# Shorter slot lists, packed overflow and three dense blocks first, in the expert product of a one-core kernel

## The chip, the cores and the metric

One core of one Trainium2 chip runs the kernel. The metric is the device time of one execution in microseconds (us); "before" is the median of three timed runs, and one further execution was taken by the hardware profiler. Engines are named as the profile names them: PE (TensorE matmul), DVE (VectorE), ACT (ScalarE), POOL (GpSimd), SP (SyncE, here a queue of transfers).

## The reference

256 tokens of width 2048 pass one layer: an attention and recurrence sub-layer, then the sub-layer that matters here, PEER, which retrieves experts (16,384 of them, each one row of u and one row of v):

```python
def peer(h, w_q, sub_keys, u, v):
    ...
    gate = jax.nn.softmax(best_s, axis=-1)
    def block(args):
        hb, eb, gb = args
        ub = u[eb]
        vb = v[eb]
        act = jax.nn.gelu(jnp.einsum('td,ted->te', hb, ub).astype(jnp.float32), approximate=False) * gb
        return jnp.einsum('te,ted->td', act.astype(vb.dtype), vb)
```

Each token has 8 heads with 16 experts each, so of the 16,384 gated hidden values of a token at most 128 are not zero. A gated residual and a last RMSNorm follow.

## The kernel before, in words

The kernel computes PEER densely first and sparsely second. Experts are numbered (j, p): 128 blocks j of 128 partitions p. For each j, `stacked_block` makes the hidden values of all 256 tokens on PE, and `u_evac` (L1055) adds two halves (ACT `low`, DVE `low`) and applies GELU. `gating` multiplies the blocks j < NS by the gates, which earlier code scattered into a table, and writes them to `hid` in DRAM; blocks j >= NS stay in SBUF in `late` and are gated there (`late_gates`, L1227).

A chunk is one pair (j, p): one hidden row of 256 tokens (two tiles of 128) and one row of v with 2048 values. `make_lists` (L1106) builds for each partition p two lists of j whose chunk isn't zero: list 0 has those of tile 0, with those that both tiles use in front; list 1 those of tile 1 alone. DVE does it in turns of eight (MAX, MATCH_REPLACE, then `decode` into rows of `hid` and `w_v`). Lists have SLOTS places. What is over goes to further chunks by a place computed over all partitions: `ob` holds counts of what is over, a matmul with a triangle of ones (`ps_list`, L1187) sums them over partitions, and `spilling` (L1341) writes each item of overflow to its place in a table in DRAM by a scatter.

`second_product` (L1365) multiplies. Its items come from `plan` (L1401): "feed" items are whole late blocks whose v rows come by the queue of weight loads; a double is one slot of list 0 for both tiles; a single is one slot for one tile; "over" is a packed chunk; two dense late blocks come last. `fetch` (L1294) loads slot n of all 128 partitions at once by two indirect transfers from POOL, `hr` (128x256 of `hid`) and `v` (128x2048 of `w_v`); AHEAD = 4 items are in flight over five buffers. `parts_of` splits values in a high part (ACT `vh`, `ap`) and a low one (DVE `vl`, `ap`); `v_products` then does three matmuls of 128x512 for each of four column groups, so 12 for one tile and 24 for two:

```python
    def v_products(out, tt, q, parts, start, stop, keep=lambda i: i):
        ...
        keep(mm(out, ap[:, 0, t], vh[:, w], start, False))
        keep(mm(out, ap[:, 0, t], vl[:, w], False, False))
        keep(mm(out, ap[:, 1, t], vh[:, w], False, stop))
```

All sums stay in eight banks `out..` of PSUM until `finish` (L1455) does the last two items, residual, norm and store. One scatter is issued per item (L1388), since each engine runs its instructions in program order and POOL has the gathers too. If overflow doesn't fit, a flag `bad` makes all 128 dense blocks run as a fallback. NS = 124, SLOTS = (56, 35), BOTH = 29 and OVER = (16, 12, 10) give 2 feed items, 29 doubles, 62 singles, 2 "over" and 2 dense: 33 of 24 matmuls and 64 of 12.

## Time and profile before

| | us |
|---|---|
| median of 3 runs (2154.59, 2158.49, 2158.61) | 2158.49 |
| the profiled execution | 2151.07 |
| its span in the trace | 2149.2 |
| PE busy | 2035.7 (95%) |
| DVE busy | 1644.7 (77%) |
| ACT busy | 1068.9 (50%) |
| POOL busy | 1025.7 (48%) |

The mean granted clock of PE was 0.98. Busy times are sums over the whole span: the second product fills about its last sixth, from 1763 us on, and the work before it is the attention sub-layer, the routing and the 128 blocks of hidden values. An engine that is busy most of the time isn't thereby the one that is waited for; that is read by stage. Row starts below are microseconds from the start of the span, and a row with "[9.94 <-ACT ap L225]" says how long its engine sat idle before it and which instruction ended that.

### The profile page before, as it was taken

What the parts mean: (1) busy time and instruction counts of PE and PEld (TensorE: products, weight loads), DVE (VectorE), ACT (ScalarE), POOL (GpSimd) and SP (SyncE); (2) the same over time, 40 slices, a digit from 0 to 9 for tenths busy, and PEclk for the clock granted to TensorE, in tenths of its full rate; (3) what the DMA queues carried; (4) which work ended last, traced back from release to release, by engine and by line L of the source; (5) the groups of instructions that cost most, each with busy time, mean ns of one, the idle gap of its engine ahead of it and who ended that gap; (6) DMA issues with size and microseconds to landing.
All of it is one profiled execution on the core that took longest, in us unless ns stands there. A gap on an engine that the chain in (4) does not pass through costs nothing. (4 is left out here: it accounts for less than half of the span.)

```text
span 2149.2 us, 34359 instructions
## 1 busy us (share of the span) xinstructions
PE 2035.7 (95%) x12916; PEld 1841.5 (86%) x12916; DVE 1644.7 (77%) x2538; ACT 1068.9 (50%) x1559; POOL 1025.7 (48%) x663
## 2 busy tenths in 40 slices
PE   6989999999999999999999999998999989999996
PEld 6988998779999999899888888887888778886885
DVE  7899888878675888887999666687558776765687
ACT  3433334455645445444666555543554445654575
POOL 3333422224420001218777688777871026777763
PEclk8999999999999999999999999999999999999998
DMA  6878778676677899857777898899879979999994
GB/s 252 310 267 317 258 254 288 207 239 210 214 236 263 312 334 326 310 176 183 180 181 186 231 262 257 249 324 291 223 212 360 319 261 334 282 261 268 386 382 178
DMA packets 208832, 568.65 MB, mean 265 GB/s; under 512 B 57585, under 2 KB 89489, under 8 KB 191633
## 3 DMA queue, kind: packets, MB, share of 16 engines
q1 hardware_dynamic: 147248, 441.38, 59.5%
q0 software_dynamic: 58928, 123.94, 21.5%
q8 instruction: 103, 1.69, 0.3%
q10 hardware_dynamic: 2482, 1.07, 0.2%
q14 instruction: 71, 0.58, 0.1%
HBM read 544.95 MB, written 38.06 MB: 271 GB/s over the span
## 5 line engine op out<-in xcount | busy, mean ns | idle before, releaser
L90 ACT ACTIVATE hi<-raw 128x1024 fp32r<-128x1024 f32 x550 | 580.9, 1058 | 686.0 <-PE ps_w L120 270.6
L94 DVE TENSOR_TENSOR lo<-raw,hi 128x1024 fp32r<-128x1024 f32 x506 | 652.5, 1292 | 256.0 <-ACT hi L90 254.3
L120 PE MATMUL ps_w<-h,hi 128*128 128x512 f32 (+1 forms) x2560 | 811.9, 373 | 12.7 <-ACT hi L90 7.4
L120 PE MATMUL ps_w<-h,lo 128*128 128x256 f32 x2304 | 649.5, 282 | 10.5 <-DVE lo L94 10.5
L921 POOL DMA_INDIRECT gtab<-gate,addr x256 | 508.7, 1987 | 174.9 <-issue 70.9
L120 PEld LDWEIGHTS ps_w<-h,hi 128*128 128x128 f32 x2560 | 465.0, 189 | 100.1 <-ACT hi L90 9.2
L120 PEld LDWEIGHTS ps_w<-h,lo 128*128 128x128 f32 x2304 | 437.0, 190 | 17.4 <-DVE lo L94 16.6
L120 PE MATMUL out<-vh,ap 128*128 128x512 f32 x1008 | 313.3, 391 | 2.8 <-ACT vh L225 2.8
L226 DVE TENSOR_TENSOR vl<-v,vh 128x1024 fp32r<-128x1024 f32 x190 | 224.6, 1224 | 72.7 <-ACT vh L225 70.7
L94 POOL TENSOR_TENSOR lo<-raw,hi 128x1024 fp32r<-128x1024 f32 x44 | 117.6, 2673 | 294.1 <-ACT hi L90 294.1
L120 PEld LDWEIGHTS out<-vh,ap 128*128 128x128 f32 x1008 | 189.5, 188 | 44.4 <-ACT vh L225 5.3
L225 ACT ACTIVATE vh<-v 128x1024 fp32r<-128x1024 f32 x190 | 189.8, 1047 | 72.4 <-DMA v<-w_v,index 67.7
L120 PE MATMUL set<-h1hi,hi 128*128 128x256 f32 x768 | 212.3, 291 | 13.5 <-ACT h1hi L242 7.1
L120 PE MATMUL set<-h1hi,lo 128*128 128x256 f32 x768 | 198.5, 293 | 22.1 <-DVE lo L94 18.9
L120 PE MATMUL set<-h1lo,hi 128*128 128x256 f32 x768 | 212.8, 288 | 0.9 <-DVE h1lo L244 0.9
L120 PE MATMUL out<-vl,ap 128*128 128x512 f32 x504 | 197.6, 392 | 4.9 <-DVE vl L226 4.9
L186 DVE SCALAR_TENSOR_TENSOR raw<-raw,cond 128x1024 f32<-128x1024 f32 x96 | 134.2, 1404 | 49.6 <-DMA raw<-w_ada 45.9
L120 PEld LDWEIGHTS set<-h1hi,hi 128*128 128x128 f32 x768 | 150.1, 198 | 16.6 <-ACT h1hi L242 7.3
L120 PEld LDWEIGHTS set<-h1hi,lo 128*128 128x128 f32 x768 | 141.2, 199 | 26.6 <-DVE lo L94 23.1
L120 PE MATMUL ps_w<-h1hi,hi 128*128 128x256 f32 x528 | 150.8, 286 | 3.0 <-ACT hi L90 3.0
L120 PE MATMUL ps_w<-h1hi,lo 128*128 128x256 f32 x528 | 150.3, 285 | 1.9 <-DVE lo L94 1.9
L120 PEld LDWEIGHTS set<-h1lo,hi 128*128 128x128 f32 x768 | 150.9, 197 | 1.2 <-DVE h1lo L244 1.2
(356 smaller groups left out, 3196.6 us busy)
## 6 DMA issues: line engine op xcount, KB each, us to landing
raw<-w_u SPq DMA_DIRECT2D x256, 512.0 KB, 4.4
raw<-w_sets SPq DMA_DIRECT2D x96, 512.0 KB, 5.4
raw<-w_ada SPq DMA_DIRECT2D x96, 512.0 KB, 5.1
raw<-w_t SPq DMA_DIRECT2D x66, 512.0 KB, 4.6
ada<-w_ada SPq DMA_DIRECT2D x32, 1024.0 KB, 8.3
raw<-w_s SPq DMA_DIRECT2D x32, 512.0 KB, 4.6
gtab<-zeros_d SPq DMA_DIRECT2D x32, 512.0 KB, 5.5
raw<-w_up SPq DMA_DIRECT2D x32, 512.0 KB, 4.7
```

The source lines that it names most:

```text
L90: self.nc.scalar.activation(hi, raw, AF.Copy)
L94: i = eng.tensor_sub(lo, raw, hi.bitcast(F32))
L120: return nc.tensor.matmul(out, lhsT, rhs, start=start, stop=stop, skip_group_check=True)
L186: return nc.vector.scalar_tensor_tensor(w, w, 1.0, cond[:, k0:k0 + n], op0=ALU.mult, op1=ALU.mult, accum_out=col)
L225: nc.scalar.activation(hi, v, AF.Copy)
L226: (lo_eng or nc.vector).tensor_sub(lo, v, hi.bitcast(F32))
L921: return nc.gpsimd.indirect_dma_start(out=gtab[tt].rearrange("p (x o) -> (p x) o", o=1), out_offset=bass.IndirectOffsetOnAxis(ap=addr[:, t ...
```

## The change

NS becomes 125, so three late blocks are left, and all three are "feed" items at the front; no dense block stands at the end. Lists get 72 and 48 places (WIDE), but only the first 52 and 28 are slots that are fetched directly, and BOTH falls to 20. What is over is packed into 10 further chunks (MORE = 3 for tile 0, 7 for tile 1). The items are 3 feed, 20 doubles (the last two at the very end) and 70 singles (10 of them packed): 23 of 24 matmuls and 70 of 12, and 90 gathered chunks where there were 93.

The 38 scatters and their table go. In their place the whole lists are stored once to `table` in DRAM (from SP), and for each packed chunk and partition the source is found by products: `hot` marks, for each partition, which overflow places its items take (compares on DVE against an iota, both kept in the not yet used `ye`); 17 small matmuls (`picked`, into bank `ps_sel`) add up, for each place, partition and slot; DVE turns this into rows of `table` (`oplace`), and `picking` gathers 128 index pairs per packed chunk from POOL, one gather per item. Since `ps_sel` needs a bank, bank `out13` is taken only after it, and six matmuls of the first two feed items are held until then. The lists themselves are made after `ps_list`, not before. `late_gates` loads its gates from SP, not POOL.

```diff
-NS = 124
-SLOTS = (56, 35)
-BOTH = 29
-OVER = (16, 12, 10)
+NS = 125
+SLOTS = (52, 28)
+BOTH = 20
+WIDE = (72, 48)
+MORE = (3, 7)
...
+
+    index_all = kp.tile([P, sum(WIDE), 2], U32, name="index_all")
+    index = [index_all[:, 0:WIDE[0], :], index_all[:, WIDE[0]:, :]]
+    oplace = kp.tile([P, sum(MORE)], U32, name="oplace")
+    oindex = kp.tile([P, sum(MORE), 2], U32, name="oindex")
...
-    over = dram.tile([256 + P * sum(OVER), 2], U32, name="over")
+    ROWS = P * sum(WIDE)
+    table = dram.tile([ROWS + 1, 2], U32, name="table")
...
+
+        place = w1(sum(MORE), "place")
+        for c in range(sum(MORE)):
+            nc.vector.tensor_scalar(place[:, c:c + 1], tcol, 128.0 * (c - (c >= MORE[0]) * MORE[0]) - ROWS, None, op0=ALU.add)
+        begin = lists.tile([P, 3, 2], F32, name="begin")
+        nc.vector.memset(begin, 1.0)
+        for i, n in enumerate((SLOTS[0], WIDE[0] + SLOTS[1], BOTH)):
+            nc.vector.tensor_scalar(begin[:, i, 0:1], tcol, float(sum(WIDE)), float(n), op0=ALU.mult, op1=ALU.add)
...
-        turn_of(0, 0)
-        turn_of(0, 8)
-        decode(0, 0, 16)
-        yield 3000
...
-        nc.vector.tensor_mul(key[:, 1, :], alone, rev)
-        turn_of(1, 0)
-        decode(1, 0, 8)
-        yield 1700
-        for c in (8, 16, 24):
-            turn_of(0, 8 + c)
-            turn_of(1, c)
-            decode(0, 8 + c, 16 + c)
-            decode(1, c, c + 8)
-            yield 2500
...
         nc.vector.tensor_reduce(cnt[:, 0:1], b[:, 0, :], axis=AX.X, op=ALU.add)
         nc.vector.tensor_reduce(cnt[:, 1:2], alone, axis=AX.X, op=ALU.add)
         nc.vector.tensor_reduce(cnt[:, 2:3], both, axis=AX.X, op=ALU.add)
         ob = w1(4, "ob")
...
+        for i, n in enumerate(WIDE):
+            nc.vector.tensor_scalar(t1[:, i:i + 1], cnt[:, i:i + 1], float(n), None, op0=ALU.is_gt)
+        nc.vector.tensor_add(ob[:, 3:4], t1[:, 0:1], t1[:, 1:2])
+        yield 3000
         yield LATER
         ps = bank("ps_list")
         mm(ps[:, 0:4], tri, ob, True, True)
@@ -1189,55 +1164,93 @@
         nc.scalar.activation(off, ps[:, 0:8], AF.Copy)
         state["counted"] = True
-
-        for i in range(2):
-            for c in range(40 - 8 * i, SLOTS[i] + OVER[i], 8):
-                turn_of(i, c)
-                yield 650
-            decode(i, 40 - 8 * i, SLOTS[i] + OVER[i])
...
+        def turn_of(i, c0):
...
+        turn_of(0, 0)
+        turn_of(1, 0)
+        yield 3200
...
+        wide = 128 * max(MORE)
+        iota_w = state["space"][:, 0:wide]
+        pin(nc.gpsimd.iota(iota_w, pattern=[[1, wide]], base=0, channel_multiplier=0, allow_small_or_imprecise_dtypes=True))
...
+        end = w1(3, "end")
+        nc.vector.tensor_add(end, off[:, 0:3], ob[:, 0:3])
+        nc.vector.tensor_sub(begin[:, :, 0], begin[:, :, 0], off[:, 0:3])
+        hot = []
+        for i in range(3):
+            n = 128 * MORE[i > 0]
+            t = state["space"][:, 1024 * (i + 1):1024 * (i + 1) + n]
+            nc.vector.tensor_scalar(t, iota_w[:, 0:n], off[:, i:i + 1], None, op0=ALU.is_ge)
+            nc.vector.scalar_tensor_tensor(t, iota_w[:, 0:n], end[:, i:i + 1], t, op0=ALU.is_lt, op1=ALU.mult)
+            hot.append(t)
             yield 1000
...
+        state["hot"] = (hot, begin, place)
...
+        for i in range(2):
+            nc.vector.tensor_scalar(tot[:, i:i + 1], off[:, 4 + i:5 + i], 128.0 * MORE[i], None, op0=ALU.is_gt)
...
-        for i, n in enumerate(OVER):
...
-            nc.vector.tensor_add(oplace[i], at, dump)
+        yield 500
+        for c in range(8, WIDE[0], 8):
+            if c < WIDE[1]:
+                turn_of(1, c)
+                yield 1000
+            turn_of(0, c)
             yield 1300
-        state["placed"] = True
+        pin(nc.sync.dma_start(table[0:ROWS].rearrange("(p c) x -> p c x", p=P), index_all))
+        state["tabled"] = True
+
+    def picked(ps):
+
+        hot, begin, place = state["hot"]
+        for c in range(sum(MORE)):
+            ones = [(0, c)] if c < MORE[0] else [(1, c - MORE[0]), (2, c - MORE[0])]
+            for i, (l, n) in enumerate(ones):
+                pin(mm(ps[:, 2 * c:2 * c + 2], hot[l][:, 128 * n:128 * n + 128], begin[:, l, :],
+                       i == 0, i == len(ones) - 1))
+        got = lists.tile([P, sum(MORE), 2], F32, name="got")
+        nc.scalar.activation(got.rearrange("p c x -> p (c x)"), ps[:, 0:2 * sum(MORE)], AF.Copy)
+        nc.vector.tensor_mul(place, place, got[:, :, 1])
+        nc.vector.tensor_add(place, place, got[:, :, 0])
+        nc.vector.tensor_scalar(oplace, place, float(ROWS), None, op0=ALU.add)
 
     def late_gates():
 
-        while state["gated"] < 2:
+        while state["j"] < NS - 8:
...
+        for tt in range(2):
+            after_all(pin(nc.sync.dma_start(lateg[:, tt, :, :], gtab[tt][:, 128 * NS:])), tt)
...
         if j == 122:
-            feed.add([a["w_v"][n][:, 1024 * u:1024 * u + 1024] for n in range(NS, 126) for u in range(2)])
+            feed.add([a["w_v"][n][:, 1024 * u:1024 * u + 1024] for n in range(NS, 128) for u in range(2)])
...
+    state["space"] = ye.rearrange("p z d -> p (z d)")
...
-    def spilling():
...
-        for i, n in enumerate(OVER):
-            for k in range(n):
-                src = index[i][:, SLOTS[i] + k, :] if i < 2 else index[0][:, BOTH + k, :]
-                one = pin(nc.gpsimd.indirect_dma_start(
-                    out=over, out_offset=bass.IndirectOffsetOnAxis(ap=oplace[i][:, k:k + 1], axis=0),
-                    in_=src, in_offset=None))
...
-        got = pin(nc.sync.dma_start(oindex, over[0:256].rearrange("(c p) x -> p c x", p=P)))
...
+    def picking():
+
+        while not state["tabled"]:
+            yield
+        for c in range(sum(MORE)):
+            pin(nc.gpsimd.indirect_dma_start(
+                out=oindex[:, c, :], out_offset=None, in_=table,
+                in_offset=bass.IndirectOffsetOnAxis(ap=oplace[:, c:c + 1], axis=0)))
+            state["picked"] = True
+            yield
     def second_product(items, listed=False):
-        outs = [[bank(f"out{tt}{q}") for q in range(4)] for tt in range(2)]
+        sel = bank("ps_sel") if listed else None
+        outs = [[bank(f"out{tt}{q}") if not listed or tt == 0 or q < 3 else None for q in range(4)] for tt in range(2)]
...
-        spill = spilling() if listed else iter(())
+        pick = picking() if listed else iter(())
+        held = []
...
                 bg.run(700)
-                if state["placed"]:
-                    next(spill, None)
+                next(pick, None)
...
             for hf in range(2):
                 for tt in now[2]:
                     for q in (2 * hf, 2 * hf + 1):
-                        v_products(outs[tt][q], tt, q, now, (tt, q) in fresh, False)
-                        fresh.discard((tt, q))
+                        if outs[tt][q] is None:
+                            held.append((now, tt, q))
+                        else:
+                            take(now, tt, q)
+            if listed and n == 1:
+                while "hot" not in state:
+                    bg.run(1e9)
+                picked(sel)
+                outs[1][3] = bank("out13")
+                for h in held:
+                    take(*h)
         last = [nxt, parts_of(got.popleft())]
         finish(outs, last)
...
         two = [(1, n, (1,)) for n in range(SLOTS[1])]
-        single = []
+        single = two[:8]
+        two = two[8:]
         while one or two:
             for l in (one, two):
                 if l:
                     single.append(l.pop(0))
+        single += [("more", n, (int(n >= MORE[0]),)) for n in range(sum(MORE))]
         double = [(0, n, (0, 1)) for n in range(BOTH)]
-        dense = [("all", n, (0, 1)) for n in range(NS, 128)]
-        items, acc = [("feed", n, (0, 1)) for n in range(NS, 126)], 0.0
-        for d in double:
+        for d in double[:-2]:
             items.append(d)
-            acc += len(single) / len(double)
+            acc += len(single) / (len(double) - 2)
             while acc >= 1.0 and single:
                 items.append(single.pop(0))
                 acc -= 1.0
-        return items + single + [("over", n, (n,)) for n in range(2)] + dense[-2:]
+        return items + single + double[-2:]
```

On PE the place between the first product's last blocks (`ps_w`) and the second's first (`out`). Before:

```order
L120 MATMUL ps_w<-h_9294,hi 128x512
L120 MATMUL ps_w<-h_9294,lo 128x256
L120 MATMUL ps_list<-ob,tri 128x4
L120 MATMUL ps_list<-ob,ones_l 128x4
L120 MATMUL out_18153<-hi,ap 128x512
L120 MATMUL out_18153<-lo,ap 128x512
```

Now:

```order
L121 MATMUL ps_w<-h_9294,hi 128x512
L121 MATMUL ps_w<-h_9294,lo 128x256
L121 MATMUL ps_list<-ob,tri 128x4
L121 MATMUL ps_list<-ob,ones_l 128x4
L121 MATMUL ps_w<-h_9293,hi 128x512
L121 MATMUL ps_w<-h_9293,lo 128x256
```

The two matmuls of `ps_list` stood behind block 127; now they stand behind block 126, ahead of block 127.

On ACT the same place (`hi` are weights' high parts, `low` and `late` the last blocks' hidden values, `ap` and `vh` high parts for the second product, `off` the copy of `ps_list`, `got` that of `ps_sel`). Before:

```order
L1059 ACTIVATE low<-ps_w 128x256
L1190 ACTIVATE off<-ps_list 128x8
L1065 ACTIVATE late<-low 128x256
L225 ACTIVATE vh<-v 128x1024 x2
L225 ACTIVATE ap<-late 128x256 x2
L225 ACTIVATE ap<-hr 128x256
```

Now:

```order
L226 ACTIVATE ap<-late 128x256
L1068 ACTIVATE late<-low 128x256
L226 ACTIVATE ap<-late 128x256
L1165 ACTIVATE off<-ps_list 128x8
L91 ACTIVATE hi<-raw 128x1024 x2
L1062 ACTIVATE low<-ps_w 128x256
L91 ACTIVATE hi<-raw 128x1024
L1068 ACTIVATE late<-low 128x256
L226 ACTIVATE vh<-v 128x1024 x6
L91 ACTIVATE hi<-raw 128x1024
L226 ACTIVATE ap<-late 128x256
L1237 ACTIVATE got<-ps_sel 128x20
```

The split of the first late blocks moved ahead of every gathered `vh`; that of the last one and one `hi` of its v rows stand behind six `vh`.

On POOL the first gathers, now:

```order
L1196 IOTA ye 128x896
L1321 DMA hr<-hid,index_all 128x256
L1321 DMA v<-w_v,index_all 128x2048
L1321 DMA hr<-hid,index_all 128x256
L1321 DMA v<-w_v,index_all 128x2048
L1360 DMA oindex<-table,oplace 128x2
L1321 DMA hr<-hid,index_all 128x256
L1321 DMA v<-w_v,index_all 128x2048
L1360 DMA oindex<-table,oplace 128x2
```

Three gathered chunks stand ahead of the iota, so five ahead of the first index gather; the scatters, which stood one ahead of each of 38 items, are gone.

## Rows read from the trace of the kernel before

**Rows 1.** The page, part 1: busy us, share of the span and instructions of each engine.

```profile
PE 2035.7 (95%) x12916; PEld 1841.5 (86%) x12916; DVE 1644.7 (77%) x2538; ACT 1068.9 (50%) x1559; POOL 1025.7 (48%) x663
```

**Rows 2.** Table by stage: window; its us; busy us of each engine; PEclk, DMA share, GB/s.

```profile
1763.00:1834.00 71.00, 70.95 (x301) 58.25 (x302) 51.39 (x87) 39.77 (x54) 46.85 (x41) 0.96 0.93 337
1834.00:1934.00 100.00, 100.00 (x443) 82.81 (x442) 64.97 (x75) 55.34 (x74) 78.31 (x70) 1.00 0.99 273
1934.00:2020.00 86.00, 80.70 (x344) 63.58 (x343) 52.02 (x59) 45.00 (x60) 66.16 (x57) 1.00 0.98 305
```

**Rows 3.** Instructions that write tile out, on PE: duration ns min/median/max, first and last start.

```profile
L120 PE MATMUL out<-vh,ap x1008: 387/389/796, 1774.0 to 2132.4; 128*128 128x512 f32 x168
L120 PE MATMUL out<-vl,ap x504: 387/389/632, 1774.2 to 2132.2; 128*128 128x512 f32 x168
```

**Rows 4.** Timeline of PE, 2042 to 2056: start, us, instruction.

```profile
2042.45 0.39 PE L120 MATMUL out<-vl,ap 128*128 128x512 f32 x1
...
2054.01 0.39 PE L120 MATMUL out<-vl,ap 128*128 128x512 f32 x1
```

**Rows 5.** Timeline of ACT, 2090 to 2106: start, us, instruction, idle before and its releaser.

```profile
2093.79 2.02 ACT L225 ACTIVATE vh<-v 128x1024 fp32r<-128x1024 f32 x2 [0.68 <-DMA v<-w_v,index]
...
2102.39 2.01 ACT L225 ACTIVATE vh<-v 128x1024 fp32r<-128x1024 f32 x2 [0.66 <-DMA v<-w_v,index]
```

**Rows 6.** Timeline of POOL, 1822 to 1830 and 1976 to 1990.

```profile
1826.71 1.02 POOL L1347 DMA_INDIRECT over<-index,oplace  x1 [0.30 <-issue]
...
1984.50 1.00 POOL L1347 DMA_INDIRECT over<-index,oplace  x1 [0.31 <-issue]
...
1987.08 1.01 POOL L1307 DMA_INDIRECT v<-w_v,index  x1 [0.30 <-DVE vl L226]
1988.39 1.00 POOL L1347 DMA_INDIRECT over<-index,oplace  x1 [0.30 <-issue]
```

**Rows 7.** What PE waited for from 1826 to 1992: us in total, times, longest.

```profile
PE out L120 <- DVE vl L226: 4.1, 6, 0.8
PE out L120 <- ACT vh L225: 0.9, 1, 0.9
```

**Rows 8.** Timeline of PE, 1746.9 to 1770.

```profile
1747.06 0.39 PE L120 MATMUL ps_w<-h,hi 128*128 128x512 f32 x1
...
1752.61 0.28 PE L120 MATMUL ps_list<-ob,tri 128*128 128x4 f32 x2
1752.75 0.36 PE L120 MATMUL ps_list<-ob,ones_l 128*128 128x4 f32 x2
1763.05 0.80 PE L120 MATMUL out<-hi,ap 128*128 128x512 f32 x1 [9.94 <-ACT ap L225]
...
1768.34 0.41 PE L120 MATMUL out<-hi,ap 128*128 128x512 f32 x1
```

**Rows 9.** Timeline of ACT, 1747 to 1764.

```profile
1760.69 2.00 ACT L225 ACTIVATE vh<-v 128x1024 fp32r<-128x1024 f32 x2 [3.57 <-DMA v<-w_v,index]
1762.60 0.71 ACT L225 ACTIVATE ap<-late 128x256 fp32r<-128x256 f32 x2
```

**Rows 10.** Timeline of DVE, 1748 to 1762.

```profile
1749.76 0.41 DVE L1060 TENSOR_TENSOR low<-low,ps_w 128x256 f32<-128x256 f32 x1
...
1751.09 1.21 DVE L94 TENSOR_TENSOR lo<-raw,hi 128x1024 fp32r<-128x1024 f32 x1
1752.21 0.09 DVE L1144 MATCH_VALUE_LOAD key<-lst,key 128x8 f32 x1
```

**Rows 11.** Transfers by issue: engine, operation, count, KB each, median us to landing.

```profile
out<-ye SPq DMA_DIRECT2D x8, 256.0 KB, 2.7
...
v<-w_v,index POOLq DMA_INDIRECT x91, 8.8
```

**Rows 12.** Timeline of PE, 2111 to 2150.

```profile
2116.38 2.17 PE L120 MATMUL out<-vh,ap 128*128 128x512 f32 x4 [1.91 <-ACT vh L225]
...
2132.39 0.39 PE L120 MATMUL out<-vh,ap 128*128 128x512 f32 x1
```

More of the change, by code (lines that the diff above doesn't have):

```diff
@@ new lines, in make_lists @@
+        lst = [w1(n, f"lst{i}") for i, n in enumerate(WIDE)]
+        def turn_of(i, c0):
+            c1 = c0 + 8
+            l = lst[i][:, c0:c1]
+            nc.vector.max(l, key[:, i, :])
+            if c1 < WIDE[i]:
+                nc.vector.match_replace(key[:, i, :], l, key[:, i, :], 0.0)
+            if i == 0:
+                nc.vector.tensor_scalar(w[:, c0:c1], l, 128.0, -128.0, op0=ALU.is_gt, op1=ALU.mult)
+                nc.vector.tensor_add(w[:, c0:c1], l, w[:, c0:c1])
+                l = w[:, c0:c1]
+            nc.vector.tensor_scalar(index[i][:, c0:c1, 0], l, -1.0, hbase, op0=ALU.mult, op1=ALU.add)
+            nc.vector.tensor_scalar(index[i][:, c0:c1, 1], l, -128.0, vbase, op0=ALU.mult, op1=ALU.add)
+            state["listed"][i] = c1
@@ L1300, in fetch @@
             bg.run(1e9)
-        assert kind != "over" or state["spilled"]
+        assert kind != "more" or state["picked"]
         v = vraw.tile([P, D], F32, name="v")
@@ L1304, in fetch @@
             h = hraw.tile([P, T], F32, name="hr")
-            ix = (oindex if kind == "over" else index[kind])[:, n, :]
+            ix = (oindex if kind == "more" else index[kind])[:, n, :]
             for t_, rows, z in ((h, hid_rows, 0), (v, v_rows, 1)):
@@ L1339, in v_products, with take @@
         keep(mm(out, ap[:, 1, t], vh[:, w], False, stop))
-    def spilling():
-        sent = []
-        for i, n in enumerate(OVER):
-            for k in range(n):
-                src = index[i][:, SLOTS[i] + k, :] if i < 2 else index[0][:, BOTH + k, :]
-                one = pin(nc.gpsimd.indirect_dma_start(
-                    out=over, out_offset=bass.IndirectOffsetOnAxis(ap=oplace[i][:, k:k + 1], axis=0),
-                    in_=src, in_offset=None))
-                if sent:
-                    tc.declare_no_dep(one.ins, group="spill", reason="no two places that count are the same")
-                tc.add_to_no_dep_group("spill", one.ins)
-                sent.append(one)
-                yield
-        yield
-        yield
-        got = pin(nc.sync.dma_start(oindex, over[0:256].rearrange("(c p) x -> p c x", p=P)))
-        for one in sent:
-            tc.add_manual_dep(got.ins, one.ins.name,
-                              mybir.DependencyInfo(mybir.DependencyClass.Sync, mybir.DependencyReason.DATA),
-                              reason="all of what is over")
-        state["spilled"] = True
-        yield
+    def picking():
[7 more added lines that the diff above has]
+            yield
     def second_product(items, listed=False):
-        outs = [[bank(f"out{tt}{q}") for q in range(4)] for tt in range(2)]
+        sel = bank("ps_sel") if listed else None
+        outs = [[bank(f"out{tt}{q}") if not listed or tt == 0 or q < 3 else None for q in range(4)] for tt in range(2)]
         fresh = {(tt, q) for tt in range(2) for q in range(4)}
+        def take(now, tt, q):
+            v_products(outs[tt][q], tt, q, now, (tt, q) in fresh, False)
+            fresh.discard((tt, q))
         AHEAD = 4
```

82 lines of the change are left out of this document (22 added, 60 removed).

## The prediction

> **What bounds the kernel now.** I read the page first, then the table by stage, then single engines. The page [rows 1] says that TensorE (PE) is busy for 95% of the span. An average hides stages, so the second look is the table of windows over the second product, the only part that the change rewrites: PE is busy 70.95 of 71 us, then 100.00 of 100, then 80.70 of 86 [rows 2]. So PE sets the pace there with one leak of about 5 us, although the DMA share reads 0.93 to 0.99 in all of these rows. The third look counts PE's work: 1008 + 504 products of gathered or loaded chunks [rows 3], and 48 more of the two feed blocks, 1560 in all, which agrees with the plan (33 items of 24 and 64 of 12). At full clock 51 products take 2054.01 − 2042.45 = 11.56 us, 0.2268 us each [rows 4]. The 0.39 us in a row is a product's length in the pipeline, not its price.
>
> **Term 1, fewer products: −38.1 us.** The new plan has 3 feed blocks and 20 doubles (24 products each) and 70 singles (12 each): 552 + 840 = 1392, 168 fewer. 168 × 0.2268 = 38.1 us. This is gained in full only if PE stays the bound. Per gathered chunk the transfers are 1,048,576 B of v and 131,072 B of hidden, 1.18 MB. Where ACT waits for nothing but v, three chunks take 2102.39 − 2093.79 = 8.60 us, 2.87 each, or 411 GB/s [rows 5]. Singles are densest at the start of the new order, 3.9 to a double: that costs PE 24 + 46.8 = 70.8 products, 16.1 us, and the transfers 4.9 × 2.87 = 14.1 us, so PE keeps a margin of 2 us, and more later, where doubles are denser. Only the run of about 26 singles near the end costs PE 12 × 0.2268 = 2.72 us against 2.87: 0.15 × 26 = 3.9 us at most, less what has been loaded ahead by then. I take 0 and keep +4 as a bound.
>
> **Term 2, the scatters: −5.0 us.** Between 1826.7 and 1989.4 POOL issues a scatter, an hr gather and a v gather for each item. One such turn takes 1988.39 − 1984.50 = 3.89 us [rows 6], as much as an item costs PE, and PE waits there seven times for split chunks, 4.1 + 0.9 = 5.0 us in all [rows 7]. Without the scatter a turn is two issues, 2.58 us. The ten picks that replace them have the same length (taken from the scatter's 1.00 + 0.31 us), so for ten items the old pace stays; 10 × (3.89 − 16.1 / 4.9) = 6 us of the lead of the gathers is used up, and four chunks fetched ahead cover it. I take −5.0; bounds are 0 (the waits have another cause) and −5.0.
>
> **Term 3, the start of the second product: +1 us.** Before, block 127 runs from 1747.06 to 1752.61, PE idles 9.94 us for the split late block, and the first 12 products run at the lower of the two clock levels (5.29 us from 1763.05 to 1768.34, 2.6 more than 12 × 0.2268) [rows 8]. ACT was held there: it split a gathered v (2.00 us at 1760.69) before the late block [rows 9]. By 1763.05 + 5.29 + 44 × 0.2268 = 1778.3 PE has done 56 products. In the new order of instructions the late blocks are split on ACT ahead of every gathered chunk. That takes the 9.94 us away. Three waits come instead. ps_list now stands ahead of block 127 on PE and needs ob, which stands six short rows behind low of block 126 on DVE; that one was at 1749.76 [rows 10], so ob is there at about 1751 and PE idles 3.9 us with block 127 and all else queued behind. If the clock drops as it did behind the 9.94 us, 2.6 us more: block 127 ends near 1759. Then 42 products of blocks 125 and 126 (9.5 us, to 1769). Then ps_sel, which needs the compares `hot`: from low of 126 to the last of them DVE has 86 rows: three subtractions of 128x1024 (1.12 us from one start to the next, [rows 10]), 25 list operations of about 0.2 to 0.26, six compares of 384 or 896 columns (under the 1.21 us of a 1024 wide row, about 0.7 on average) and some 50 small ones near 0.1, 19 us together, so about 1769 as well. For 17 products of ps_sel I take 0.22 us each (ps_list's two begin 0.14 us apart and end 0.50 after the first start [rows 8]): 3.7 us, to 1773; the six held back to 1774. Block 127 is last: its hi stands on ACT behind six vh of three gathered chunks, its lo on DVE behind six vl, near 1778. PE reaches 56 products at about 1779.3: +1. Bounds: −12.5 (the idle time and slow clock both vanish) and +10 (one more stall like that of before).
>
> **Term 4, POOL held by the first pick: 0.** The picks need the table, and that needs every list. On POOL the first pick stands behind the fifth gathered chunk. DVE writes the last index some ten 1.12 us rows behind the compares, near 1780; the store of 128 rows of 1920 B I take at 4 us, between the 2.7 us of a 256 KB store and 8.8 of a gather [rows 11]: 1784. Pick, hr and v then take 1.3 + 2.6 to issue, 8.8 to land, 2 to split: 1799. PE wants the sixth chunk after 72 products of feed blocks and 84 of the first five chunks; the 100 behind the 56 already counted take it from 1779.3 to 1802. Covered by 3 us; bound +5.
>
> **Term 5, the end: 0.** PE stalls 1.91 us before the first of the last two items and then runs slowly for some products, 4 us in all [rows 12]; now two doubles stand there in place of two dense blocks. They are fetched in the same turn of buffers, so I leave it; bounds −4 (the stall goes) and none above, as the run of singles has its own bound. The 16.4 us from 2132.39 + 0.39 to the end of the span are `finish`, untouched.
>
> The rest I cost at nothing: the two gate loads of the late blocks go from POOL's queue to SP's some ten blocks before they are needed; the table's store stands on SP ahead of loads that only `finish` reads; the iota stands on POOL between gathers, inside the time that term 4 counts. Without that cover each would add its own 1 to 2 us.
>
> Sum: −38.1 − 5.0 + 1 + 0 + 0 = −42.1 us. The profiled execution took 2151.07 (span 2149.2 and 1.9 around it), 7.4 below the median of 2158.49; so 2109.0 on its scale and **2116.4 us** on the median's. A measurement here tells about 0.2% (4 us) from no change.
>
> **Rivals.**
> *Transfers bind (2124).* For: the DMA share is 0.93 to 0.99 throughout, and the stretch from 1763 to 1834 moved only 337 GB/s [rows 2]. At that rate a chunk costs 3.5 us and 90 cost 315, just PE's 1392 × 0.2268 = 316; with the first chunk there at 1760.7 and POOL held some 10 us by the first pick the last lands at 2086, then split and 24 products, 2 + 5.4, and the end stall of 4: PE ends at 2098 instead of 2090, +8. Against: 411 GB/s is shown in rows 5. The Trainium skill, "DMA: Bandwidth & Descriptors", section "Where 436 GB/s comes from", has a rule that speaks for this rival: a core's share of HBM, about 358 GB/s, binds HBM to SBUF transfers; an estimate from it is 3.3 us per chunk and 297 us for all. The trace disagrees: 411 GB/s from HBM over 8.6 us [rows 5].
> *The start stalls once more (2126).* DVE's list work, moved between the last blocks and the first chunks, is late by as much as PE's old gap: +10. For: DVE reads as busy without a break around low of block 126, and three waits in a row need it. Against: the sum above already pays each once.
> *The table is late (2163), the slower side.* The pick at the head of POOL's queue holds every later gather until the table has landed. Each us behind 1787 is a us of PE. Before, the last placing was done only in time for the first scatter at 1826.71 [rows 6]. If the lists of the change end no earlier, and the store and the next gather follow, the loss is 40 + 7 us: 2163. It decides from 1787 + 42 = 1829 on. Against: in the new order the list turns stand ahead of nearly all vl on DVE.
> *The fallback runs (about 2810).* If a list is longer than its 72 or 48 places, or 384 or 896 overflow places don't do, 128 dense blocks follow: 128 × 24 × 0.2268 = 697 us. Counted from the reference's inputs, the longest lists are 66 and 43 and the overflow 159 and 581, so it should not.
>
> **How the numbers follow.** Forecast 0.62; transfers bind 0.18; start stalls 0.14; table late 0.04; fallback 0.02. The first three are all faster: 0.94. The late table gives slower from its far end and about the same from its near end: 0.02 same, 0.02 slower, and the fallback 0.02: 0.04 slower. Range: downward the stalls of terms 3 and 5 gone (−12.5 and −4) make 2100 together, which needs both; I take 2103. Upward it holds both faster rivals and their price plus the +4 or +5 of terms 1 and 4: 2131.
>
> **What would show it.** Right: 1392 products of the second product, no `over` rows on POOL, PE without gaps between about 1800 and 2085, the end of PE near 2090. Wrong: a PE gap behind ps_list or ps_sel over 5 us; hr gathers on POOL that stand behind the first pick past 1787; ACT waiting for v in the interleaved stretch at a pace above PE's own 16.1 / 4.9 = 3.29 us per chunk; rows of dense blocks after `finish`.

## The result and the profile after

| | before | changed |
|---|---|---|
| median of 4 runs, us | 2158.55 | 2121.55 |
| lowest and highest, us | 2154.59, 2163.12 | 2117.36, 2132.62 |
| profiled execution, us | 2151.07 | 2117.36 |
| its span, us | 2149.2 | 2115.6 |
| PE: end of block 126, us from the span's start | 1747.07 | 1755.47 |
| PE: start of the last product | 2132.39 | 2098.66 |
| between the two ("the second part") | 385.3 | 343.2 |

The ratio is 0.9831, interval [0.9801, 0.9861]: 36.5 us faster, between 30 and 43; the two medians themselves are 37.0 us apart. The forecast was 2116.4 (2103 to 2131) on the median and −42.1 us on the profiled scale. Between the two profiled executions the whole span differs by 33.6 us only, but the second part, the stretch that the sum was about, by 385.3 − 343.2 = 42.1. The other 8.4 us lie ahead of the end of block 126; 5.4 of them are there already at PE's first product of the PEER sub-layer (910.8 and 916.2), up to which the two programs are the same. In the profiles of this study the end of block 126 lay between 1747.1 and 1760.3, and in two long executions at 1771.9 and 1777.9. So for a change in the last sixth of a kernel the two marks on PE tell more than the span, and they are used below. The end of block 126 is the start of its last pair, 1755.12 here, plus the 0.35 us that a pair takes.

The page of the changed kernel, part 1, answers to [rows 1]:

```profile
PE 2005.2 (95%) x12782; PEld 1814.1 (86%) x12782; DVE 1636.9 (77%) x2543; ACT 1058.7 (50%) x1549; POOL 982.2 (46%) x628
```

PE's share is the same 95%; its busy time fell by 30.5 us. The table by stage of the changed kernel, columns as in [rows 2]:

```profile
1765.00:1800.00 35.00, 33.53 (x151) 27.62 (x151) 26.23 (x82) 13.77 (x21) 15.29 (x14) 0.90 0.73 275
1800.00:1850.00 50.00, 47.14 (x203) 36.90 (x202) 34.48 (x40) 29.84 (x41) 39.80 (x34) 1.00 0.90 334
1850.00:1900.00 50.00, 50.00 (x223) 41.39 (x221) 41.38 (x49) 35.56 (x49) 39.94 (x34) 1.00 1.00 393
...
2050.00:2080.00 30.00, 30.00 (x134) 24.82 (x134) 25.71 (x31) 22.48 (x31) 19.55 (x19) 1.00 1.01 409
2080.00:2100.00 20.00, 17.45 (x74) 13.34 (x72) 18.03 (x22) 11.47 (x20) 7.42 (x6) 1.00 0.15 58
```

From 1850 to 2080 PE is never idle, while transfers moved 393 GB/s early in that stretch and 409 late. PE loses time in the first rows and the last. What counts there is products, not idle time: in 1800 to 1850 there are 203, worth 203 × 0.2268 = 46.0 us, so 4 us are lost, although the busy column shows 47.14. Read so, the stretch 1934 to 2020 of before [rows 2] lost 86 − 344 × 0.2268 = 8.0 us, not the 5.0 that its waits add up to [rows 7].

Products by operands, on PE of the changed kernel, answering to [rows 3]:

```profile
L121 PE MATMUL out<-vh,ap x880: 387/389/499, 1791.0 to 2098.7; 128*128 128x512 f32 x176
L121 PE MATMUL out<-vl,ap x440: 387/389/499, 1791.2 to 2098.4; 128*128 128x512 f32 x147
L121 PE MATMUL out<-hi,ap x48: 388/394/774, 1767.1 to 1794.4; 128*128 128x512 f32 x48
L121 PE MATMUL out<-lo,ap x24: 392/399/628, 1767.3 to 1794.2; 128*128 128x512 f32 x24
```

880 + 440 + 48 + 24 = 1392, as planned. The timeline of PE, the rows that end a gap or open a part:

```profile
1755.12 0.39 PE L121 MATMUL ps_w<-h,hi 128*128 128x512 f32 x1
...
1759.36 0.36 PE L121 MATMUL ps_list<-ob,tri 128*128 128x4 f32 x2 [3.73 <-DVE ob L1158]
...
1767.07 0.39 PE L121 MATMUL out<-hi,ap 128*128 128x512 f32 x1
...
1776.89 0.50 PE L121 MATMUL out<-lo,ap 128*128 128x512 f32 x1 [1.27 <-DVE lo L95]
...
1778.39 5.31 PE L121 MATMUL ps_sel<-begin,ye 128*128 128x2 f32 x34
1783.57 2.48 PE L121 MATMUL out<-hi,ap 128*128 128x512 f32 x5
1785.85 0.63 PE L121 MATMUL out<-lo,ap 128*128 128x512 f32 x1
...
1788.05 1.20 PE L121 MATMUL out<-hi,ap 128*128 128x512 f32 x4 [0.19 <-ACT hi L91]
...
1832.20 0.73 PE L121 MATMUL out<-vh,ap 128*128 128x512 f32 x2 [0.99 <-ACT vh L226]
...
1843.40 2.13 PE L121 MATMUL out<-vh,ap 128*128 128x512 f32 x8 [1.50 <-ACT vh L226]
...
2087.51 0.50 PE L121 MATMUL out<-vh,ap 128*128 128x512 f32 x1 [0.83 <-ACT vh L226]
2088.77 0.50 PE L121 MATMUL out<-vl,ap 128*128 128x512 f32 x1 [0.76 <-DVE vl L227]
...
2098.66 0.39 PE L121 MATMUL out<-vh,ap 128*128 128x512 f32 x1
```

The start is as foreseen in kind: PE waits 3.73 us for `ob` in front of ps_list, then runs block 127 until 1767.07 (7.3 us from the end of ps_list, where 5.55 were spent before [rows 8]), waits for a split block, runs ps_sel for 5.31 us, and takes 2.28 us for the five products behind it (1783.57 to 1785.85), twice their usual 1.13. Then there are gaps at 1832 and 1843 that the forecast did not have, and waits of 0.83 and 0.76 us at the end.

POOL and ACT of the changed kernel around those gaps:

```profile
1775.78 1.88 POOL L1321 DMA_INDIRECT v<-w_v,index_all  x1 [0.31 <-issue]
1793.88 0.95 POOL L1360 DMA_INDIRECT oindex<-table,oplace  x1 [16.22 <-DMA table<-index_all]
1795.14 0.94 POOL L1321 DMA_INDIRECT hr<-hid,index_all  x1 [0.30 <-issue]
```

```profile
1826.51 2.01 ACT L226 ACTIVATE vh<-v 128x1024 fp32r<-128x1024 f32 x2 [3.90 <-DMA v<-w_v,index_all]
...
1831.09 2.00 ACT L226 ACTIVATE vh<-v 128x1024 fp32r<-128x1024 f32 x2 [2.38 <-DMA v<-w_v,index_all]
```

POOL sat 16.22 us in front of the first index gather, waiting for the table. Each of the next items is one index gather dearer on POOL, and at 1826 ACT has nothing left that was fetched ahead: it waits 3.90 and 2.38 us for v.

### The profile page after: what moved, and what is told of

Same layout as the page of the kernel before. It is cut to its first block, busy times and chain, and to the rows that moved or that the text cites. A ratio compares the mean times of both kernels' runs of the same rounds, so it can differ in the third digit from the quotient of the medians.

```text
span 2115.6 us, 34021 instructions
## 1 busy us (share of the span) xinstructions
PE 2005.2 (95%) x12782; PEld 1814.1 (86%) x12782; DVE 1636.9 (77%) x2543; ACT 1058.7 (50%) x1549; POOL 982.2 (46%) x628
## 5 line engine op out<-in xcount | busy, mean ns | idle before, releaser
L121 PEld LDWEIGHTS ps_w<-h,lo 128*128 128x128 f32 x2304 | 437.7, 190 | 18.3 <-DVE lo L95 17.7
L121 PE MATMUL out<-vh,ap 128*128 128x512 f32 x880 | 272.7, 390 | 3.7 <-ACT vh L226 3.7
L227 DVE TENSOR_TENSOR vl<-v,vh 128x1024 fp32r<-128x1024 f32 x180 | 212.9, 1224 | 38.9 <-ACT vh L226 36.8
L121 PEld LDWEIGHTS out<-vh,ap 128*128 128x128 f32 x880 | 164.7, 188 | 40.1 <-ACT vh L226 6.2
L226 ACT ACTIVATE vh<-v 128x1024 fp32r<-128x1024 f32 x180 | 179.9, 1047 | 37.2 <-DMA v<-w_v,index_all 30.8
L121 PE MATMUL out<-vl,ap 128*128 128x512 f32 x440 | 171.7, 390 | 0.8 <-DVE vl L227 0.8
L121 PEld LDWEIGHTS set<-h1hi,hi 128*128 128x128 f32 x768 | 149.6, 197 | 15.8 <-ACT h1hi L243 6.4
L121 PE MATMUL ps_w<-h1lo,hi 128*128 128x256 f32 x528 | 151.5, 287 | 0.0
```

What stands on the lines that cost most here:

```text
L121: return nc.tensor.matmul(out, lhsT, rhs, start=start, stop=stop, skip_group_check=True)
L226: nc.scalar.activation(hi, v, AF.Copy)
L227: (lo_eng or nc.vector).tensor_sub(lo, v, hi.bitcast(F32))
```

## The experiments

All of them are measured by the second part, from the end of block 126 to the last product, in one profiled execution each. "Excess" is what the time from the first product to the last holds beyond 0.2268 us per product.

| kernel | products | second part, us | 56th product, from the end of block 126 | excess | median (runs), ratio to before [interval] |
|---|---|---|---|---|---|
| before | 1560 | 385.3 | 31.5 | 15.8 | |
| changed | 1392 | 343.2 | 33.6 | 16.1 | 2121.55 (4), 0.9831 [0.9801, 0.9861] |
| late picks | 1392 | 337.3 | 33.3 | 10.2 | 2111.06 (4), 0.9797 [0.9727, 0.9867] |
| counts behind block 127 | 1392 | 339.7 | 22.1 | 18.3 | 2117.44 (4), 0.9815 [0.9752, 0.9878] |
| 29 doubles | 1500 | 365.0 | 33.2 | 13.6 | 2136.09 (10), 0.9912 [0.9877, 0.9946] |
| before without scatters | 1560 | 378.3 | 31.6 | 8.9 | 2149.90 (10), 0.9973 [0.9944, 1.0001] |
| one sel product | 1392 | 345.2 | 33.0 | 16.8 | 2117.47 (1) |
| late picks, counts inside block 127 | 1392 | 341.8 | 36.0 | 19.2 | 2123.40 (4), 0.9842 [0.9771, 0.9912] |
| the same, iota first | 1392 | 334.9 | 28.7 | 12.2 | 2113.52 (4), 0.9780 [0.9723, 0.9837] |
| before, dense blocks first | 1560 | 389.9 | 33.9 | 17.3 | 2166.15 (10), 1.0029 [0.9994, 1.0064] |
| changed, again | 1392 | 355.8 | 32.6 | 27.4 | 2122.56 (6), 0.9765 [0.9732, 0.9798] |
| iota first, again | 1392 | 348.8 | 27.8 | 26.2 | 2123.08 (6), 0.9771 [0.9736, 0.9807] |
| changed, third | 1392 | 355.5 | 32.7 | 27.3 | 2127.01 (6), 0.9767 [0.9727, 0.9807] |
| late picks, again | 1392 | 348.6 | 33.9 | 20.4 | 2125.94 (6), 0.9759 [0.9716, 0.9803] |

**Products.** BOTH = 29 brings back products without touching gathers.

```diff
-BOTH = 20
+BOTH = 29
```

> The changed kernel with BOTH = 29 again: the same 90 gathered chunks and the same index gathers, but 29 doubles and 61 singles, so 1500 products in place of 1392. Theory A (PE sets the pace, each product costs 0.2268 us): 108 x 0.2268 = 24.5 us longer than the changed kernel, about 2146. Theory B (transfers or gathers set the pace, equal in both): under 10 us longer.

```profile
L121 PE MATMUL out<-vh,ap x952: 387/389/628, 1786.2 to 2116.1; 128*128 128x512 f32 x191
L121 PE MATMUL out<-vl,ap x476: 389/389/793, 1786.4 to 2115.9; 128*128 128x512 f32 x159
```

With the feed blocks' 72 that is 1500. The second part grew by 365.0 − 343.2 = 21.8 us, near A's 24.5 and far from B. Counted in bins of 20 us from the end of block 126, the excess of 4.4 between 60 and 100 us falls to 0.4 (likely because PE takes the chunks more slowly there, which leaves the gathers their lead), and the end costs 1.7 more. So a product is worth its 0.2268 us; the 168 that were saved carry the change. On the median A's "about 2146" was missed: 2136.09, only 14.5 us over the changed kernel's first median, between A and B. The verdict rests on the second part, not on the median.

**Scatters.** Out of the kernel before, which then leaves what is over out of its sum:

```diff
-                one = pin(nc.gpsimd.indirect_dma_start(
-                    out=over, out_offset=bass.IndirectOffsetOnAxis(ap=oplace[i][:, k:k + 1], axis=0),
-                    in_=src, in_offset=None))
```

> The kernel before without its 38 scatters: what is over is left out of the sum (the two packed chunks read padding). Theory A (three issues of 1.3 us per item on POOL delay the gathers): the excess of PE between 1930 and 1990, 7.7 us over 0.2268 per product, goes entirely, about 8 us less than before, near 2150 on the median. Theory B (transfers are short there, DMA share 0.98): under 2 us less.

The table by stage, a window that answers to 1934 to 2020 of before within some 2 us:

```profile
1940.00:2026.00 86.00, 86.00 (x381) 71.21 (x380) 56.48 (x64) 48.63 (x65) 42.86 (x44) 1.00 0.80 297
```

381 products in 86 us: nothing is lost any more, at 297 GB/s where before had 305. Without the scatters POOL has a third issue less per item, and the DMA engines have less to do (share 0.80, not 0.98 [rows 2]); the edit takes away both. That POOL was the short one is read from the kernel before: with its 57 instructions and the 0.30 us in front of each, POOL was occupied for 66.16 + 57 × 0.30 = 83.3 of the 86 us [rows 2, 6]. 8.3 us of excess went; the end gave 1.3 back, on PE's timeline a longer stall than [rows 12]:

```profile
2117.80 0.75 PE L120 MATMUL out<-vh,ap 128*128 128x512 f32 x2 [3.22 <-ACT vh L225]
```

In sum −7.0 us in the second part. The median of 10 runs is 5.8 us lower, with an interval that just reaches 1.

**The held POOL.** In the changed kernel, picks from item 24 on:

```diff
-                next(pick, None)
+                if n >= 24: next(pick, None)
```

> The changed kernel, but the first of the ten index gathers is issued from item 24 on and no longer at the sixth gathered chunk. In the changed kernel POOL sat idle 16.22 us (until 1793.88) before its first index gather, and PE then waited for split chunks between 1832 and 1845, 4.4 us lost in all. Theory A (the held gather and the slow turns that follow use up the lead of the gathers): POOL's idle row of 16 us goes, PE has no gap over 0.3 us between 1800 and 1850, 4.4 us less (ratio to the changed kernel 0.998). Theory B (the single chunks stand too densely there and the transfers bind): the gaps stay within 1 us of 4.4 in sum, no change of time.

All waits of PE over the second part that the profile lists:

```profile
PE ps_list L121 <- DVE ob L1158: 3.7, 1, 3.7
PE out L121 <- DVE lo L95: 1.3, 1, 1.3
PE out L121 <- DVE vl L227: 0.8, 1, 0.8
```

Between 1800 and 2078 no gap is left. The second part is 337.3 us, 5.9 less than in the changed kernel: 4.4 in the middle, 1.2 at the end, 0.3 at the start. POOL idles here too, 11.81 us until 1784.97, but for a free buffer and not for the table; its sixth hr goes out 34.0 us after the end of block 126, not 39.7. A holds for the stretch; the medians' intervals overlap.

**The wait for the counts.** ps_list behind block 127:

```diff
-        yield LATER
+        while state["j"] < 128: yield LATER
         ps = bank("ps_list")
```

> The changed kernel, but ps_list (the sums of the overflow counts) is issued on PE behind block 127, as in the kernel before, and no longer ahead of it. Theory A (PE's wait for ob is a pure loss): the 3.73 us gap before ps_list and the lower clock of block 127 behind it (7.2 us instead of 5.55) go, the compares on DVE end at about the same time since list turns fill DVE anyway, and PE reaches the 56th product of the second part 4 to 5 us earlier counted from the end of block 126 (28.5 to 29.5 us instead of 33.5). Theory B (the start is bound by DVE's list work, whatever the order on PE): the wait comes back in front of ps_sel or of the products of block 127, less than 1.5 us gained.

```profile
1781.84 0.96 PE L121 MATMUL out<-hi,ap 128*128 128x512 f32 x3 [2.75 <-ACT hi L91]
1785.54 0.79 PE L121 MATMUL out<-lo,ap 128*128 128x512 f32 x1 [2.74 <-DVE lo L95]
...
1790.80 5.70 PE L121 MATMUL ps_sel<-begin,ye 128*128 128x2 f32 x26 [0.48 <-DVE ye L1207]
```

More than ps_list moved: other products went ahead of ps_sel on PE, which makes the mark at the 56th product (22.1) useless here. PE's timeline shows the 3.73 us gone and 2.75, 2.74 and 0.48 back, in front of block 127's v rows and inside ps_sel; ps_sel's last 26 passes took 5.70 us at the lower clock (granted 0.50 from 1785 to 1796). In the first 40 us after block 126 the time that isn't products of the second part is 23.9 us, where the changed kernel has 20.9: 3 us worse. That the second part is 3.5 shorter nevertheless comes from the middle (4.4 less; that PE was late enough there for the gathers is the likely reason, not tested) and from the end (2.1 less). So B for the start.

A middle way puts ps_list behind 8 of block 127's 16 pairs, with late picks:

```diff
-        yield 3000
-        yield LATER
+        yield 0
+        while state["j"] < 127: yield LATER
         ps = bank("ps_list")
-        mm(ps[:, 0:4], tri, ob, True, True)
+        pin(mm(ps[:, 0:4], tri, ob, True, True))
```

(and `pin` on the rest of ps_list and on block 127's pairs, to keep that order).

> The changed kernel with late picks (as in the run with index gathers from item 24 on) and with ps_list issued on PE in the middle of block 127, behind 8 of its 16 pairs. Theory A (only the position on PE was wrong): the wait for ob shrinks from 3.73 to about 1 us, the lower clock of block 127 goes, the compares end when they did: from the end of block 126 to the last product 333 us, against 337.3 with late picks alone. Theory B (the start is bound by what comes behind, the compares or the split of block 127's v rows): the wait comes back there, 336 to 338 us.

```profile
1753.31 0.36 PE L121 MATMUL ps_list<-ob,tri 128*128 128x4 f32 x2 [0.84 <-DVE ob L1159]
...
1772.51 2.07 PE L121 MATMUL out<-hi,ap 128*128 128x512 f32 x4 [5.94 <-ACT hi L91]
...
1779.79 4.81 PE L121 MATMUL ps_sel<-begin,ye 128*128 128x2 f32 x34
```

The wait for `ob` fell to 0.84 us as meant, and 5.94 us came back in front of block 127's first v rows: 341.8, 4.5 worse than late picks alone. It is B in kind, and worse than B's 336 to 338; that only the place on PE was wrong is refuted.

To this the next version adds the iota ahead of the gathers, moved to where `ye` is made, so that `hot` can be computed before most list turns:

```diff
     state["space"] = ye.rearrange("p z d -> p (z d)")
+    pin(nc.gpsimd.iota(state["space"][:, 0:128 * max(MORE)], pattern=[[1, 128 * max(MORE)]], base=0, channel_multiplier=0, allow_small_or_imprecise_dtypes=True))
```

> As the run with ps_list inside block 127, and the iota stands on POOL ahead of the first gathers, so that the compares stand on DVE ahead of most list turns. Theory: the compares then end before the first 42 products of the second part, ps_sel waits for nothing, and the stretch from the end of block 126 to the last product is 331 to 333 us; if DVE's list work or block 127's v rows bind, 336 or more.

```profile
1762.99 0.36 PE L121 MATMUL ps_list<-ob,tri 128*128 128x4 f32 x2 [0.96 <-DVE ob L1159]
...
1776.48 3.85 PE L121 MATMUL ps_sel<-begin,ye 128*128 128x2 f32 x34
1782.14 0.79 PE L121 MATMUL out<-hi,ap 128*128 128x512 f32 x1 [1.80 <-ACT ap L226]
```

ps_sel waits for nothing and comes 17.4 us after block 126, not 22.9. The forecast of 331 to 333 was missed with 334.9, as 1.80 us came back behind ps_sel, but it is the shortest second part of all: 8.3 under the changed kernel, 3.6 of it in the first 60 us, 3.4 between 60 and 100, where late picks act, and 1.2 at the end.

**The price of ps_sel.** One product with zeros in place of 17, so what is over is left out:

```diff
+        pin(mm(ps[:, 0:2 * sum(MORE)], hot[2][:, 0:128], nothing, True, True))
...
-                pin(mm(ps[:, 2 * c:2 * c + 2], hot[l][:, 128 * n:128 * n + 128], begin[:, l, :],
-                       i == 0, i == len(ones) - 1))
```

> The changed kernel with the 17 one-hot products of ps_sel replaced by a single product with zeros (the ten packed chunks then read padding, so what is over is left out); the waits for the compares stay. In the changed kernel ps_sel took PE 5.3 us and the next ten products ran at the lower clock, 2 us more. Theory A (these 7 us are a price of the one-hot products): PE reaches the 56th product 6 to 7 us earlier, 27 us from the end of block 126 instead of 33.5. Theory B (block 127's split v rows are late anyway, their hi and lo stand behind six vh and vl): PE waits for them instead, under 2 us earlier.

```profile
1757.71 0.56 PE L121 MATMUL ps_list<-ob,tri 128*128 128x4 f32 x2 [3.72 <-DVE ob L1158]
...
1776.76 0.29 PE L121 MATMUL ps_sel<-nothing,ye 128*128 128x20 f32 x2
1781.32 2.50 PE L121 MATMUL out<-hi,ap 128*128 128x512 f32 x5 [4.27 <-ACT ap L226]
```

ps_sel is down to 0.29 us, and PE waits 4.27 us behind it and then runs at the lower clock again (2.50 us for the row of five). The 56th product comes 0.6 us earlier. B: the 17 products filled a wait for `ap` of the last late block.

**Dense blocks first** alone, in the kernel before:

```diff
-        items, acc = [("feed", n, (0, 1)) for n in range(NS, 126)], 0.0
-        for d in double:
+        items, acc = [("feed", n, (0, 1)) for n in range(NS, 128)], 0.0
+        for d in double[:-2]:
...
-        return items + single + [("over", n, (n,)) for n in range(2)] + dense[-2:]
+        return items + single + [("over", n, (n,)) for n in range(2)] + double[-2:]
```

> The kernel before with its four late blocks all as feed items at the front and two doubles at the very end; lists, slots and scatters as before, 1560 products as before. Theory A (the end stall of before came from two dense blocks loaded late): the 4.7 us of excess at the end fall to about 2, as in the changed kernel, and the front stays: 2 to 3 us less than before. Theory B (the end stall is that of whatever comes last): no change at the end. If the two further feed blocks bring a new wait at the front, as three vh ahead of their hi did in the changed kernel, the sum is zero or worse.

```profile
PE out L120 <- ACT ap L225: 13.0, 1, 13.0
PE out L120 <- DVE vl L226: 6.4, 10, 0.8
PE out L120 <- ACT vh L225: 3.1, 4, 1.3
```

The end lost 0.6 in place of 4.7 us, more than A asked. But the first wait grew from 9.94 to 13.0, and behind it PE lost 14.4 us during the scatters, where 8.3 were lost before: 389.9, 4.6 longer. So A holds for the end, and the sum is worse. Alone this part of the change doesn't pay.

**Once more.** The changed kernel and the shortest version, timed side by side:

> The changed kernel once more, on the same chip as the run that follows. Its second part has no freedom: from the end of block 126 to the last product 343 us again, within 1; the part ahead of it may stand anywhere within some 10 us, as in the runs so far, and if the change has no effect on that part, five rounds give a ratio to the kernel before between 0.978 and 0.986.

> Late picks, ps_list inside block 127 and the iota first, as in the run of that name, which took 334.9 us from the end of block 126 to the last product. If its gain of 8 us on the changed kernel is that of its second part and not of a chance, 335 us again within 1.5, and a median 6 to 10 us under the changed kernel's in the same rounds.

Both missed: 355.8 and 348.8, and no gain on the median. The ratio missed too, on the fast side (0.9765): beside these runs the kernel before took 2170.06, 11.5 us more than at first, the changed kernel only 1.0 more. Timeline of ACT, changed kernel, among the last singles:

```profile
2065.34 2.01 ACT L226 ACTIVATE vh<-v 128x1024 fp32r<-128x1024 f32 x2 [3.56 <-DMA v<-w_v,oindex]
...
2068.20 2.01 ACT L226 ACTIVATE vh<-v 128x1024 fp32r<-128x1024 f32 x2 [0.66 <-DMA v<-w_v,oindex]
```

After 3.56 us of waiting for one late v the pace is the known one, (2068.20 − 2065.34) = 2.86 us per chunk, so there a single transfer came late rather than all (a wait of this length occurs once here, not twice as the next expectation has it). The table by stage:

```profile
1800.00:1850.00 50.00, 44.62 (x176) 34.19 (x175) 30.67 (x36) 26.69 (x37) 35.37 (x31) 0.90 0.80 300
...
2050.00:2070.00 20.00, 18.94 (x82) 14.91 (x81) 16.36 (x21) 13.73 (x19) 16.15 (x13) 1.00 0.92 330
```

There are 176 products from 1800 to 1850 where the first profile had 203. A third profile, on another chip, with late picks beside it:

> The changed kernel a third time, since its second part took 343.2 us in one profile and 355.8 in the next, where ACT waited 3.5 us twice for a late transfer. If late transfers are a chance of that one execution, 343 within 1.5 here; if transfers are near the bound as the second rival said, again over 345 with ACT waiting for v among the last singles.

> The changed kernel with the index gathers from item 24 on, in the same rounds as the changed kernel itself. From its profile (337.3 against 343.2 us for the second part) the median should be 4 to 8 us under that of the changed kernel; if the order of the gathers only moves the wait to other transfers, within 2 us of it.

```profile
1800.00:1850.00 50.00, 42.94 (x170) 33.22 (x169) 31.13 (x36) 26.60 (x36) 36.13 (x32) 0.90 0.81 302
...
2050.00:2070.00 20.00, 19.79 (x88) 15.81 (x86) 17.17 (x21) 14.27 (x20) 16.13 (x13) 1.00 0.99 369
```

The second alternative of the first expectation held: 355.5, with 170 products from 1800 to 1850, and 369 GB/s in place of 409 among the last singles. But ACT's waits for v are at most 2.0 us there, and most of what is lost stands elsewhere. Of the 12.6 and 12.3 us by which the second part grew in the two later profiles of the changed kernel, 5.9 and 7.5 lie between 40 and 100 us after block 126, 7.7 and 5.3 behind 280 us. In the first of these stretches ACT's long wait stands in front of a split of hidden values, not of v; the row in the third profile:

```profile
1819.35 0.31 ACT L226 ACTIVATE ap<-hr 128x128 fp32r<-128x128 f32 x1 [10.70 <-remote]
```

The profile names no instruction that ended this wait ("remote"), nor what ended ten waits of PE, mostly in the same stretch, 5.3 us together ("issue"). The second profile has 9.84 and 5.4 us of the two, the first neither. Late picks lost nothing there in the same measurement (9.8 us between 60 and 100 in the changed kernel, 0.1 with late picks), so the held POOL had a part in it; 6.0 us came back between 120 and 180.

For late picks the second part is 348.6, 6.9 shorter than the changed kernel's beside it, and for the iota version it was 7.0 shorter. Each gain of the second part thus stands in one pair of profiles from the same chip, with the first profiles (5.9 and 8.3) agreeing. The medians do not show them: 2125.94 against 2127.01, within 2 us as the second alternative had it, and 2123.08 against 2122.56. The profiled executions of these two, 2138.97 and 2144.45, are the two that ended block 126 only at 1771.9 and 1777.9. Each has one long wait there, on PE and on DVE of late picks:

```profile
1649.27 0.58 PE L121 MATMUL ps_w<-h,lo 128*128 128x256 f32 x1 [16.52 <-DVE lo L95]
```

```profile
1645.40 1.22 DVE L1099 TENSOR_TENSOR hid1a<-hid1a,gl 128x1024 f32<-128x1024 f32 x1 [18.92 <-DMA gl<-gtab]
```

DVE stood before the first gating for gates that POOL was still scattering: its last gate scatter went out at 1637.6 here and at 1644.5 in the other, between 1594 and 1628 in the twelve other profiles. Neither edit touches that: up to the end of block 126 the order of instructions on PE, DVE, ACT and POOL is the changed kernel's, and the same two kernels ended block 126 at 1751.0 and 1759.1 in their first profiles. So these 16 us vary from one execution to the next; why the scatters were slower isn't shown. No version is shown to beat the changed kernel on the median.

## Why the prediction was right, term by term

The second part shortened by 42.1 us, the forecast sum to the tenth. That it agrees so closely is luck: only the first term was right by itself, and the errors of the others, −3.3, +1.1, +4.4 and −2.3 us, cancel. The mechanism that carries the forecast, PE's pace times 168 products, is the one that the runs show.

| term | forecast | measured | from |
|---|---|---|---|
| 1, 168 products fewer | −38.1 | −38.1 | count and pitch; 29 doubles confirm the price |
| 2, scatters | −5.0 | −8.3 | excess in the bins 180 to 280 us, gone without scatters |
| 3, start | +1 | +2.1 | 56th product at 33.6, not 31.5 |
| 4, POOL held | 0 | +4.4 | excess from 60 to 100 us, gone with late picks |
| 5, end | 0 | −2.3 | excess 4.7 to 2.4 |
| sum | −42.1 | −42.2 | |

**Term 2** had the right mechanism and too small a size: it added up the waits [rows 7], which leave out the slower products around each gap. **Term 4** failed in the step that said the lead covers the hold. The first pick went out 1793.88 − 1755.47 = 38.4 us after the end of block 126, against 1784 − 1747 = 37 in the forecast, and the sixth chunk came in time. (The store has rows of 960 B, not 1920, and landed in 2.3 us, not 4; the lists were late by about as much.) Under term 2 the forecast had set down ten items at a slower turn that use up 6 us of lead; they met a lead that the hold had just emptied. The two had to be added, to each other and against one cover. **Term 3**: the wait for `ob` was 3.73 (3.9 forecast), the slower clock behind it 1.7 (2.6), ps_sel 5.31 (3.7), block 127's v rows last, all as described. ps_sel was dearer because PE's granted clock fell inside it (1.00 until 1780, 0.50 from 1782); where it stayed at 1.00, as with the iota first, ps_sel took 3.85. The parts came near their sizes, so the term's smallness wasn't luck. Of the four experiments on the start three only moved a wait; the iota version took 4.9 us off the 56th product. **Term 5**: two doubles stand at the end, fetched like any chunk, and 2.3 us went that had been put into the bounds. Dense blocks first (4.7 to 0.6) speaks for the doubles as the reason, but with 29 doubles the same end lost 4.0, so what sets the end stays open.

Of the rivals, *transfers bind* had 0.18. In the first measurement PE had no gap from 1850 to 2080 at up to 409 GB/s, so it did not come there. A rule of the Trainium skill ("DMA: Bandwidth & Descriptors", "Where 436 GB/s comes from") puts a core's share of HBM at about 358 GB/s, half of what two cores share, and lets it bind; against the measured 409, with one core running, it does not hold here. In the two later profiles the second part was over 12 us longer, at 330 and 369 GB/s in a stretch of 20 us. That is more than this rival's +8, but it isn't shown to be a bound on the rate: the pace between waits stayed at 2.86 us, and half of the loss stands where no wait for v is seen. *The start stalls once more* did not come in the change (+2.1, not +10). *The table is late* and *the fallback* did not come.

Of the signs that the prediction named, 1392 products, no `over` rows and the end of PE came (2099.1, less the 8.4 us that lie ahead: 2090.7). PE without gaps did not, and one sign of being wrong did: between the two waits at 1826.51 and 1831.09 ACT's pace was 4.58 us per chunk, above 3.29. It pointed at term 4.

The median moved by −37.0 and not by −42.1. The 5 us between are of the size by which the part ahead of block 127 wanders: three profiles with before's order there ended block 126 at 1747.1, 1749.0 and 1755.5, nine with the changed order, the two long ones aside, between 1749.5 and 1760.3. They overlap; the runs don't settle whether any of it belongs to the change. In the two later measurements the medians moved by −47.5 (2170.06 to 2122.56) and −48.6 us (2175.61 to 2127.01), more than forecast, although the changed kernel's second part was 12 us longer there. The kernel before has no profile from these chips, so where it lost more isn't known, and the term by term account holds for the first pair of profiles only.

## What to carry over

Where one engine sets the pace, count its instructions times the pitch from row to row, window by window; the remainder is what all waits cost, and idle columns and tables of waits show only some of it. Two delays that draw on the same lead (a hold, then a slower pace) are added before they are held against it. Work at a seam between two phases is judged by the last thing that the seam needs: in three of four trials here, taking away the wait that shows only uncovered the next one.

## What the runs showed that was not expected

The changed kernel, with medians from 2121.55 to 2127.01, has a second part of 343 us in one profile and 355 to 356 in two others from two chips. Seen there are one v that came 3.56 us late and waits that the profile ties to no instruction; the cause is open. Small products cost more than their size: 34 passes of 128x2 took 3.85 us where the granted clock stayed at 1.00 (0.113 us each, half of a 128x512 product), 5.31 where it fell to 0.50 on the way, and 26 of them 5.70 at 0.50. Behind them in the changed kernel five products took 2.28 us where 1.13 would do.
